# Two-layer hybrid encoder: the gate's first 1024 columns, not 512, with tokens on partitions

## The chip, the core and the metric

The kernel runs on one core of a Trainium2 chip. Its time is the device time of one execution in microseconds, of which the median of three is given; beside it one execution was recorded by the profiler. The core has a matrix engine (TensorE, "PE" in the profile, with its weight loads apart as "PEld"), VectorE ("DVE"), ScalarE ("ACT"), GpSimd ("POOL") and SyncE ("SP"), which here only issues DMAs.

## The reference, cut to what matters

Two layers, each of three sub-layers on a residual stream of 256 tokens by 1024: token mixing, cross-attention into 256 memory tokens, and a gated feed-forward with a depthwise convolution of width 3 over the tokens. The change is in the third:

```python
def conv_ffn(h, w_up, conv_w, conv_b, w_down):      # h 256x1024, w_up 1024x5632, w_down 2816x1024
    a = h @ w_up
    a = conv3(a, conv_w) + conv_b                   # along the tokens, each column by itself
    g, u = jnp.split(a, 2, axis=-1)                 # gate: columns 0..2815, value: 2816..5631
    return (jax.nn.gelu(g, approximate=True) * u) @ w_down
...
h = rms_norm(x, ffn_pre_g[l])
x = x + rms_norm(conv_ffn(h, ...), ffn_post_g[l])
```

## The kernel before

All matrix products are done on split numbers: a weight or an activation is held as a high part (`wh`, `hTH`) and a low part (`wl`, `hTL`), and a product is the sum of three, high by high, high by low and low by high. `wunit` loads 512 KB of weights into a `raw` buffer; ScalarE writes the high part (L139), VectorE the low part (L140). There are six buffers each of `raw`, `wh` and `wl`, so a unit's parts can be made only when the unit six before it has been used up.

`hT` is the normed input turned, with features on partitions: 8 pieces of 128 features by 256 tokens, high and low. The tokens are in two blocks of 128, called block 0 and block 1. At the end of the sub-layer before, `nat_full` finishes block 0, norms it (`add_and_norm`, `prenorm`) and turns it (`raw_T`, L204) while block 1 is still in the product; then the same for block 1.

The feed-forward's up-projection comes in two forms.

- **Tokens on partitions** (`product`, `nat_chunk`, `mm_nat`; L270, L272, L274): 512 columns of the gate at a time. A piece of `hT` of one block is the stationary operand, 512 weight columns move. One block takes 24 matmuls of 512 columns. It needs one block alone, so block 0 can be done before block 1 is turned. The result has tokens on partitions, and the convolution wants them along the free axis, so `first_up` copies it to SBUF (L144) and turns it with four PE transposes a block (L918) into two accumulators, `first[0]` and `first[1]`, of 256 columns of the gate each.
- **Columns on partitions** (the loop over `j`; L943, L944): for 256 columns of gate (`s_` = 0) or value (`s_` = 1), 16 pairs of matmuls: the high weights against high and low tokens at once (512 columns moving), the low weights against the high tokens (256). It needs both blocks. ScalarE (L945) and VectorE (L946) add the two halves into an SBUF tile.

The loop has 11 steps, `j` = 0, 2, ... 20, of a gate half and a value half. At `j` = 0 and 2 the gate half is ready in `first`, so TensorE does the value half alone. For each half the convolution follows: one ScalarE instruction (L950) and two VectorE instructions (L952, L953) for each 128 columns, then gelu (L955), the product of the halves (L956) and the split for the down-projection (L139, L140 on `t`).

Accumulators are PSUM banks: four with the name `acc`, three `att`, one `fil`. Every accumulator of the up-projection is one of the four `acc`. A bank can be written again only when its last reader is done: for the loop's, L946; for `first`, the last L953 of its two.

The strings in `FFN`, one per layer, give the order in which the steps ahead of the loop are written: `uL` loads the units of the 512 columns, `uM0` and `uM1` are their products for the blocks, `e0` and `e1` are `first_up`, `cw` loads the convolution's weights and turns them (L906), `pl` and `p` load and compute a piece of the next layer's memory keys (layer 0 only; its matmuls are L270 to L279 with `fil`). A scheduler then sets the order of instructions on each engine from this, once, at build time; SP's order is that of the text. Each engine runs its own list strictly in that order, so an instruction that waits holds up all behind it on its engine.

Of the kernel before, what the change touches and what calls it, by code (L numbers as in the profile page):

```python
# [21 lines left out]
P = 128  # L22
D = 1024
S = 256
NB = S // P
# [23 lines left out]

MIX = (
# [9 lines left out]
    "g2",  # L62
    "aL aM a0 bL bM b0 A0 a1 pl B0 pr p b1 B1 A1 x1 x0 pl x2 y1 y2 y0 x3 z2 z0 y3 p g2 g0 z1 z3 pg g1 g3")
FFN = (
    "pl uL p uM0 uM1 cw e0 e1",
    "uL cw uM0 e0 uM1 e1")
BUFS = {"t4": 16, "t2": 10, "raw": 6, "w": 6, "acc": 4, "att": 3, "fil": 1, "gB": 2}

ENG = {"mrow": "A", "mT": "V", "dval": "A", "dn": "A", "dTq": "A", "dTk": "A", "kT": "A", "kn": "V",
# [5 lines left out]
def encoder(ctx, tc, a, out):  # L75
# [205 lines left out]
    def blk(b):  # L281
        return slice(b * P, (b + 1) * P)
# [108 lines left out]
    class Memory:  # L391
# [7 lines left out]
        def load(self):  # L399
            mem = a["mem"].rearrange("o (b p) d -> p (o b) d", p=P)  # L400
            self.rows = [t4() for _ in range(NB)]
            for b in range(NB):
                nc.sync.dma_start(self.rows[b], mem[:, b, :])
# [106 lines left out]
    for l in range(DEPTH):  # L510
# [406 lines left out]
                o = (i % 2) * S + b * P  # L917
                T.transpose(st.first[i // 2][:, o:o + P], an[:, blk(i)], ident)  # L918

        load("u", w, 0, 512, 2, None)  # L920
        product("u", 512, 2)
        steps.update(cw=conv_weights, e0=partial(first_up, 0), e1=partial(first_up, 1))
        issue(FFN[l], steps)
        cw, first = st.cw, st.first
        guH, guL = [], []
        for j in range(0, NF, 2):
            if j % 4 == 0:
                guH.append(t4(F32R).rearrange("p (k t) -> p k t", t=S))
                guL.append(t4(F32R).rearrange("p (k t) -> p k t", t=S))
            gu = []  # L930
            for s_ in range(2):
                if j < 4 and s_ == 0:
                    srcs = [first[j // 2][:, m * S:(m + 1) * S] for m in range(2)]
                else:


                    us = [wunit(w[k * P:(k + 4) * P, s_ * D_FF + j * P:s_ * D_FF + (j + 2) * P], 4, 256) for k in (0, 4)]
                    both = t2().rearrange("p (k t) -> p k t", t=S)
                    srcs = [both[:, m, :] for m in range(2)]
                    for m, acc in enumerate(accs()):  # L940
                        for kt in range(KD):
                            wH, wL = us[kt // 4]
                            T.matmul(acc, wH[:, kt % 4, blk(m)], hT[:, kt, :, :], start=kt == 0, stop=False)  # L943
                            T.matmul(acc[:, :S], wL[:, kt % 4, blk(m)], hTH[:, kt, :], start=False, stop=kt == KD - 1)  # L944
                        A_.activation(srcs[m], acc[:, S:], AF.Copy)  # L945
                        V.tensor_tensor(srcs[m], acc[:, :S], srcs[m], op=ALU.add)  # L946
                cv = t2().rearrange("p (k t) -> p k t", t=S)
                taps = [(m, srcs[m], s_ * NF + j + m) for m in range(2)]
                for m, src, f in taps:
                    A_.activation(cv[:, m, :], src, AF.Identity, bias=cw[:, 3, f:f + 1], scale=cw[:, 1, f:f + 1])  # L950
                for m, src, f in taps:
                    V.scalar_tensor_tensor(cv[:, m, 1:], src[:, :S - 1], cw[:, 0, f:f + 1], cv[:, m, 1:], op0=ALU.mult, op1=ALU.add)  # L952
                    V.scalar_tensor_tensor(cv[:, m, :S - 1], src[:, 1:], cw[:, 2, f:f + 1], cv[:, m, :S - 1], op0=ALU.mult, op1=ALU.add)  # L953
                gu.append(cv)
            A_.activation(gu[0], gu[0], AF.Gelu_apprx_tanh)  # L955
            V.tensor_tensor(gu[0], gu[0], gu[1], op=ALU.mult)  # L956
            split(guH[j // 4][:, j % 4:j % 4 + 2, :], guL[j // 4][:, j % 4:j % 4 + 2, :], gu[0])
# [28 lines left out]
```

## Time and profile before

| | |
|---|---|
| device time, median of 3 runs | 851.68 us (850.91 to 852.28) |
| the profiled execution: its time, its span | 851.3 us, 849.5 us |
| TensorE busy, share of the span | 98% |
| VectorE, ScalarE, GpSimd | 74%, 64%, 5% |
| memory read | 139.74 MB, 166 GB/s over the span |
| mean granted TensorE clock | 0.997 |

Matmuls overlap one another, and their ends are modelled, so TensorE's pace is read from one start to the next. The other engines' pace is read in the same way where the list is unbroken.

### The profile page before, as it was taken

The page shows a single profiled execution, that of the slowest core. Times are in us where ns is not written, and L with a number is a line of the kernel's source. Part 1 is how long each engine was busy: PE and PEld are TensorE (multiplying, and loading weights), DVE is VectorE, ACT ScalarE, POOL GpSimd, SP SyncE. Part 2 cuts the span into 40 slices and gives each one's busy share as a digit, 9 for nine tenths or more (in the row PEclk, how much of TensorE's full clock was granted, in tenths as well). Part 3 has the DMA queues.
Part 4 walks back from the last instruction along what each step waited for, and adds up shares of the span by engine and source line. Part 5 has one row for each costly group of instructions (what it writes and reads, how often), then busy time and mean ns, then how long its engine had stood idle before and what let it go on. Part 6 is the DMA issues. An engine that isn't in the chain of part 4 may idle for free.

```text
span 849.5 us, 13117 instructions
## 1 busy us (share of the span) xinstructions
PE 833.2 (98%) x4846; PEld 728.4 (86%) x4846; DVE 625.5 (74%) x1127; ACT 546.9 (64%) x1027; POOL 39.1 (5%) x65
## 2 busy tenths in 40 slices
PE   7999999999999999999999999999998999999997
PEld 5898999889888888888889989988996888888885
DVE  6798664776488999974487787548566799999543
ACT  7798663766368777763376777547636587777331
POOL 1120000100020000000010100001001000000000
PEclk9999999999999999999999999999999999999999
DMA  7873533572355667655737723256624446775531
GB/s 276 275 228 104 166 100 100 156 251 90 94 160 173 201 208 212 203 173 193 219 116 216 236 82 124 76 148 219 191 62 148 154 148 199 223 218 184 183 109 50
DMA packets 94704, 141.64 MB, mean 167 GB/s; under 512 B 5806, under 2 KB 71172, under 8 KB 94640
## 3 DMA queue, kind: packets, MB, share of 16 engines
q1 hardware_dynamic: 94368, 140.59, 52.8%
q8 instruction: 38, 0.62, 0.3%
q14 instruction: 26, 0.21, 0.1%
q0 software_dynamic: 160, 0.18, 0.1%
q10 hardware_dynamic: 112, 0.03, 0.0%
HBM read 139.74 MB, written 1.05 MB: 166 GB/s over the span
## 4 chain that ended last, share of the span: by engine, by line
PE 91%; DVE 4%; POOL 1%; issue 1%; DMA 1%; ACT 1%; SPq 0%; DVEq 0%; POOLq 0%; ACTq 0%
PE acc L943 18%; PE acc L270 13%; PE acc L272 13%; PE acc L274 13%; PE acc L944 9%; PE fil L270 2%; PE fil L274 2%; PE fil L272 2%; PE fil L277 2%; PE att L484 2%; PE fil L278 2%; PE fil L279 2%; PE acc L770 2%; PE acc L782 2%; PE acc L638 1%; PE att L204 1%
## 5 line engine op out<-in xcount | busy, mean ns | idle before, releaser
L140 DVE TENSOR_TENSOR wl<-raw,wh 128x1024 fp32r<-128x1024 f32 (+1 forms) x206 | 249.7, 1215 | 119.9 <-ACT wh L139 118.2
L139 ACT ACTIVATE wh<-raw 128x1024 fp32r<-128x1024 f32 (+1 forms) x206 | 215.6, 1051 | 129.6 <-PE acc L274 85.8
L943 PE MATMUL acc<-hT,wh 128*128 128x512 f32 x640 | 224.3, 396 | 0.0
L944 PE MATMUL acc<-hT,wl 128*128 128x256 f32 x640 | 178.8, 279 | 0.0
L943 PEld LDWEIGHTS acc<-hT,wh 128*128 128x128 f32 x640 | 120.2, 188 | 28.7
L272 PE MATMUL acc<-wl,hT 128*128 128x512 f32 (+3 forms) x384 | 134.9, 373 | 0.0
L274 PE MATMUL acc<-wh,hT 128*128 128x512 f32 (+3 forms) x384 | 134.4, 372 | 0.3 <-DVE hT L140 0.3
L270 PE MATMUL acc<-wh,hT 128*128 128x512 f32 (+3 forms) x384 | 134.7, 375 | 0.0
L944 PEld LDWEIGHTS acc<-hT,wl 128*128 128x128 f32 x640 | 120.7, 189 | 0.0
L274 PEld LDWEIGHTS acc<-wh,hT 128*128 128x128 f32 x384 | 72.7, 190 | 12.2 <-DVE hT L140 1.4
L272 PEld LDWEIGHTS acc<-wl,hT 128*128 128x128 f32 x384 | 72.6, 190 | 11.8 <-DVE wl L140 0.7
L270 PEld LDWEIGHTS acc<-wh,hT 128*128 128x128 f32 x384 | 72.3, 190 | 11.4 <-ACT hT L139 0.4
L270 PE MATMUL acc<-wh,t 128*128 128x512 f32 (+1 forms) x216 | 67.7, 387 | 0.0
L272 PE MATMUL acc<-wl,t 128*128 128x512 f32 (+1 forms) x216 | 67.5, 386 | 0.0
L274 PE MATMUL acc<-wh,t 128*128 128x512 f32 (+1 forms) x216 | 67.0, 384 | 0.0
L950 ACT ACTIVATE t<-t,cw 128x256 f32<-128x256 f32 x80 | 47.5, 595 | 13.9 <-DVE t L946 13.4
L262 ACT ACTIVATE wh<-raw,pre_cols 128x512 fp32r<-128x512 f32 (+3 forms) x80 | 43.7, 616 | 11.9 <-PE acc L274 7.8
L263 DVE SCALAR_TENSOR_TENSOR wl<-raw,pre_cols,wh 128x512 fp32r<-128x512 f32 (+3 forms) x80 | 46.1, 621 | 4.5 <-ACT wh L262 4.5
L270 PEld LDWEIGHTS acc<-wh,t 128*128 128x128 f32 x216 | 39.9, 188 | 8.2 <-issue 0.7
L274 PEld LDWEIGHTS acc<-wh,t 128*128 128x128 f32 x216 | 40.4, 188 | 7.5
L272 PEld LDWEIGHTS acc<-wl,t 128*128 128x128 f32 x216 | 40.3, 188 | 7.6 <-DVE ropeB L372 0.3
L178 POOL TENSOR_TENSOR rstd<-ms,nhalf 128x1 f32<-128x1 f32 x18 | 14.7, 819 | 605.0 <-DVE ms L176 600.4
(189 smaller groups left out, 1397.8 us busy)
## 6 DMA issues: line engine op xcount, KB each, us to landing
raw<-in_ffn_w_up SPq DMA_DIRECT2D x88, 512.0 KB, 4.6
raw<-in_ffn_w_down SPq DMA_DIRECT2D x44, 512.0 KB, 3.4
raw<-in_mem_w_kv SPq DMA_DIRECT2D x32, 512.0 KB, 3.7
raw<-in_w_in SPq DMA_DIRECT2D x20, 512.0 KB, 4.8
raw<-in_w_mix_out SPq DMA_DIRECT2D x16, 512.0 KB, 3.4
raw<-in_mem_w_q SPq DMA_DIRECT2D x16, 512.0 KB, 3.9
raw<-in_mem_w_o SPq DMA_DIRECT2D x16, 512.0 KB, 4.3
raw<-in_w_in SPq DMA_DIRECT2D x8, 384.0 KB, 4.6
```

Of the source, the lines that this page charges most:

```text
L139: return (A_.activation(h, src, AF.Copy), V.tensor_tensor(lo, src, h.bitcast(F32), op=ALU.subtract))
L140: V.tensor_tensor(lo, src, h.bitcast(F32), op=ALU.subtract))
L262: A_.activation(h[:, v], raw[:, v], AF.Copy, scale=g[:, i:i + 1])
L263: V.scalar_tensor_tensor(lo[:, v], raw[:, v], g[:, i:i + 1], h[:, v].bitcast(F32), op0=ALU.mult, op1=ALU.subtract)
L270: T.matmul(o, sH, w, start=start, stop=False)
L272: T.matmul(o, sH, w, start=False, stop=False)
L274: T.matmul(o, sL, w, start=False, stop=stop)
L277: T.matmul(o, wH, sH, start=start, stop=False)
L278: T.matmul(o, wH, sL, start=False, stop=False)
L943: T.matmul(acc, wH[:, kt % 4, blk(m)], hT[:, kt, :, :], start=kt == 0, stop=False)
L944: T.matmul(acc[:, :S], wL[:, kt % 4, blk(m)], hTH[:, kt, :], start=False, stop=kt == KD - 1)
L950: A_.activation(cv[:, m, :], src, AF.Identity, bias=cw[:, 3, f:f + 1], scale=cw[:, 1, f:f + 1])
```

## The change

The gate's columns 512 to 1023 get the first form too. They are a second chunk, called `y`: `yL`, `yM0` and `yM1` are its load and its products, `f0` and `f1` (`next_up`) copy each block's result to SBUF, where it stays in two `t2` tiles (`later`). When the loop comes to `j` = 4 and `j` = 6 it takes one `acc` bank, turns the 256 columns into it with four transposes, and the convolution reads that bank; TensorE does the value half alone there. The number of DMAs and their bytes are as before; four DMAs a layer are of 128x2x512 in place of 128x4x256.

```diff
 FFN = (
-    "pl uL p uM0 uM1 cw e0 e1",
-    "uL cw uM0 e0 uM1 e1")
+    "pl uL yL p uM0 yM0 f0 cw uM1 e0 yM1 e1 f1",
+    "uL yL cw uM0 yM0 f0 uM1 e0 yM1 e1 f1")
...
+        st.later = [None] * NB
+
+        def next_up(b):
+            st.later[b] = t2()
+            copy("up", st.later[b], st.y[b])
+
+        for i, name in enumerate("uy"):
+            load(name, w, i * 512, 512, 2, None)
+            product(name, 512, 2)
...
-                if j < 4 and s_ == 0:
-                    srcs = [first[j // 2][:, m * S:(m + 1) * S] for m in range(2)]
+                if j < 8 and s_ == 0:
+                    if j < 4:
+                        acc = first[j // 2]
+                    else:
+                        acc, = accs(1)
+                        for m in range(2):
+                            for b in range(NB):
+                                T.transpose(acc[:, m * S + b * P:m * S + (b + 1) * P], st.later[b][:, blk(j - 4 + m)], ident)
+                    srcs = [acc[:, m * S:(m + 1) * S] for m in range(2)]
                 else:
```

Lines of the changed kernel are one higher than before up to the steps named, and 16 higher in the loop: L943 and L944 become L959 and L960, L946 becomes L962, L952 and L953 become L968 and L969, L956 becomes L972; the new transposes are L948, those of `first_up` L919.

What follows is the order in which instructions stand on an engine, before and after. It is a list without times.

TensorE in layer 1, where block 1 of the normed input is turned (`att_1429`, `att_1430`); `acc_1448` and `acc_1449` are `first`, `acc_1447` is block 1's product of `u`, and `att_1444` the convolution's weights. Before:

```order
L274 MATMUL acc_1446_7153<-wh_1441_7139,hT_80 128x512
L204 MATMUL att_1429_7105<-ident_72,t4_1424_7094 128x128 x4
L918 MATMUL acc_1448_7179<-ident_72,t2_1450_7181 128x128
L204 MATMUL att_1430_7112<-ident_72,t4_1424_7094 128x128 x4
L906 MATMUL att_1444_7146<-ident_72,t2_1443_7143 128x44 x4
L918 MATMUL acc_1448_7179<-ident_72,t2_1450_7181 128x128
...
L270 MATMUL acc_1447_7154<-wh_1432_7121,hT_80 128x512
```

After, where `acc_1458` and `acc_1459` are the products of `u`, and `acc_1460` that of `y` for block 0:

```order
L275 MATMUL acc_1458_7163<-wh_1441_7125,hT_80 128x512
L273 MATMUL acc_1460_7189<-wl_1445_7132,hT_80 128x512
L205 MATMUL att_1429_7091<-ident_72,t4_1424_7080 128x128 x4
L205 MATMUL att_1430_7098<-ident_72,t4_1424_7080 128x128 x4
L907 MATMUL att_1456_7156<-ident_72,t2_1455_7153 128x44 x4
L275 MATMUL acc_1460_7189<-wh_1444_7131,hT_80 128x512
...
L275 MATMUL acc_1460_7189<-wh_1447_7137,hT_80 128x512
L271 MATMUL acc_1459_7164<-wh_1432_7107,hT_80 128x512
```

Eleven products of `y` for block 0 now stand with the turning of block 1, ten of them between it and the first product that needs it; one more stands some 20 matmuls earlier, between the first two products of `u` and the third. The transposes of `first_up` stand behind block 1's products.

VectorE in the loop of layer 1, from the last L953 (now L969) on `first[1]` to the fourth pass. Before, `acc_1473` and `acc_1474` are the value half of `j` = 2, `acc_1485` and `acc_1486` the gate half of `j` = 4:

```order
L953 SCALAR_TENSOR_TENSOR t2_1465_7288<-acc_1449_7180,cw_1445_7151,t2_1465_7288 128x255
L946 TENSOR_TENSOR t2_1472_7307<-acc_1473_7308,t2_1472_7307 128x256
L946 TENSOR_TENSOR t2_1472_7307<-acc_1474_7309,t2_1472_7307 128x256
L140 TENSOR_TENSOR wl_1493_7426<-raw_1491_7423,wh_1492_7425 128x1024
L140 TENSOR_TENSOR t4_1453_7218<-t2_1454_7219,t4_1452_7217 128x512
L952 SCALAR_TENSOR_TENSOR t2_1475_7346<-t2_1472_7307,cw_1445_7151,t2_1475_7346 128x255 x2
L953 SCALAR_TENSOR_TENSOR t2_1475_7346<-t2_1472_7307,cw_1445_7151,t2_1475_7346 128x255 x2
L946 TENSOR_TENSOR t2_1484_7371<-acc_1485_7372,t2_1484_7371 128x256
```

After, from the same point (`acc_1489` and `acc_1490` are the value half of `j` = 2, `acc_1494` the turned gate columns of `j` = 4, `acc_1503` its value half):

```order
L962 TENSOR_TENSOR t2_1488_7371<-acc_1490_7373,t2_1488_7371 128x256
L141 TENSOR_TENSOR wl_1513_7518<-raw_1511_7515,wh_1512_7517 128x1024
L141 TENSOR_TENSOR t4_1469_7282<-t2_1470_7283,t4_1468_7281 128x512
L968 SCALAR_TENSOR_TENSOR t2_1491_7410<-t2_1488_7371,cw_1457_7161,t2_1491_7410 128x255 x2
L969 SCALAR_TENSOR_TENSOR t2_1491_7410<-t2_1488_7371,cw_1457_7161,t2_1491_7410 128x255 x2
L968 SCALAR_TENSOR_TENSOR t2_1495_7428<-acc_1494_7423,cw_1457_7161,t2_1495_7428 128x255
L972 TENSOR_TENSOR t2_1481_7352<-t2_1481_7352,t2_1491_7410 128x512
L969 SCALAR_TENSOR_TENSOR t2_1495_7428<-acc_1494_7423,cw_1457_7161,t2_1495_7428 128x255
L968 SCALAR_TENSOR_TENSOR t2_1495_7428<-acc_1494_7423,cw_1457_7161,t2_1495_7428 128x255
L141 TENSOR_TENSOR t4_1469_7282<-t2_1481_7352,t4_1468_7281 128x512
L969 SCALAR_TENSOR_TENSOR t2_1495_7428<-acc_1494_7423,cw_1457_7161,t2_1495_7428 128x255
L962 TENSOR_TENSOR t2_1502_7447<-acc_1503_7448,t2_1502_7447 128x256
```

The first rows are the same; then the convolution of the turned columns comes in, and its last instruction on `acc_1494` stands behind the end of the step `j` = 2.

TensorE in the loop of layer 1, with the engines that an instruction waits for. Before, at the start of `j` = 4:

```order
L944 MATMUL acc_1474_7309<-hT_80,wl_1471_7304 128x256
L943 MATMUL acc_1485_7372<-hT_80,wh_1479_7361 128x512 [waits DVE_49]
L944 MATMUL acc_1485_7372<-hT_80,wl_1480_7362 128x256
L943 MATMUL acc_1485_7372<-hT_80,wh_1479_7361 128x512
L944 MATMUL acc_1485_7372<-hT_80,wl_1480_7362 128x256
```

After, at the start of `j` = 6 (`acc_1506` holds its turned columns, `acc_1515` its value half):

```order
L960 MATMUL acc_1504_7449<-hT_80,wl_1501_7444 128x256
L948 MATMUL acc_1506_7497<-ident_72,t2_1462_7215 128x128 [waits DVE_49]
L948 MATMUL acc_1506_7497<-ident_72,t2_1467_7279 128x128
L948 MATMUL acc_1506_7497<-ident_72,t2_1462_7215 128x128
L948 MATMUL acc_1506_7497<-ident_72,t2_1467_7279 128x128
L959 MATMUL acc_1515_7522<-hT_80,wh_1509_7511 128x512 [waits DVE_49,PE_49,Activation_49]
```

Before, `acc_1485` gets the bank that the value half of `j` = 0 had left. After, in the program as built, `acc_1515` gets the bank of `acc_1494`, `acc_1503` that of `first[1]`; in layer 0 the banks follow one another in the same way.

## Rows read from the trace of the kernel before

**Rows 1.** The page: busy time of TensorE; the chain that ended last, by engine.

```profile
PE 833.2 (98%) x4846; PEld 728.4 (86%) x4846; DVE 625.5 (74%) x1127; ACT 546.9 (64%) x1027; POOL 39.1 (5%) x65
...
PE 91%; DVE 4%; POOL 1%; issue 1%; DMA 1%; ACT 1%; SPq 0%; DVEq 0%; POOLq 0%; ACTq 0%
```

**Rows 2.** Waits of TensorE, whole span: in total, times, longest.

```profile
PE att L204 <- DVE t L196: 2.6, 3, 1.7
...
PE acc L918 <- ACT t L144: 0.2, 1, 0.2
```

**Rows 3.** Busy time by stretch: loop layer 0, turn of layer 1, loop layer 1.

```profile
259.90:373.00 113.10, 113.10 (x644) 98.17 (x643) 105.68 (x183) 85.96 (x143) 0.00 (x0) 1.00 0.64 197
...
657.50:660.20 2.70, 2.67 (x7) 2.15 (x8) 2.70 (x4) 1.40 (x4) 0.83 (x2) 0.53 0.32 105
...
672.30:784.00 111.70, 111.70 (x646) 97.63 (x645) 106.07 (x184) 86.76 (x146) 0.00 (x0) 1.00 0.65 200
```

**Rows 4.** Timeline of TensorE, layer 0, from block 1's products into the loop.

```profile
253.00 0.40 PE L270 MATMUL acc<-wh,hT 128*128 128x512 f32 x1
...
258.24 0.39 PE L274 MATMUL acc<-wh,hT 128*128 128x512 f32 x1
258.56 0.44 PE L906 MATMUL att<-ident,t 44*128 44x44 f32 x4
258.93 0.66 PE L918 MATMUL acc<-ident,t 128*128 128x128 f32 x4
...
260.21 0.39 PE L943 MATMUL acc<-hT,wh 128*128 128x512 f32 x1
...
372.57 0.40 PE L943 MATMUL acc<-hT,wh 128*128 128x512 f32 x1
```

**Rows 5.** Timeline of TensorE, layer 1, from block 0's products through the loop.

```profile
657.53 0.79 PE L274 MATMUL acc<-wh,hT 128*128 128x512 f32 x1 [0.30 <-DVE hT L140]
...
660.17 0.39 PE L274 MATMUL acc<-wh,hT 128*128 128x512 f32 x1
...
663.83 0.60 PE L204 MATMUL att<-ident,t 128*128 128x128 f32 x4
664.67 0.33 PE L918 MATMUL acc<-ident,t 128*128 128x128 f32 x1 [0.25 <-ACT t L144]
...
666.05 0.47 PE L270 MATMUL acc<-wh,hT 128*128 128x512 f32 x1
...
671.60 0.39 PE L943 MATMUL acc<-hT,wh 128*128 128x512 f32 x1
...
673.29 0.40 PE L943 MATMUL acc<-hT,wh 128*128 128x512 f32 x1
...
782.84 0.40 PE L943 MATMUL acc<-hT,wh 128*128 128x512 f32 x1
```

**Rows 6.** Timeline of VectorE, layer 1, the loop's first steps.

```profile
677.59 1.23 DVE L140 TENSOR_TENSOR wl<-raw,wh 128x1024 fp32r<-128x1024 f32 x1 [0.97 <-ACT wh L139]
...
683.29 0.68 DVE L956 TENSOR_TENSOR t<-t,t 128x512 f32<-128x512 f32 x1
683.88 0.47 DVE L953 SCALAR_TENSOR_TENSOR t<-acc,cw,t 128x255 f32<-128x255 f32 x1
684.28 0.74 DVE L946 TENSOR_TENSOR t<-acc,t 128x256 f32<-128x256 f32 x2
684.94 1.21 DVE L140 TENSOR_TENSOR wl<-raw,wh 128x1024 fp32r<-128x1024 f32 x1
686.07 0.69 DVE L140 TENSOR_TENSOR t<-t,t 128x512 fp32r<-128x512 f32 x1
686.67 0.87 DVE L952 SCALAR_TENSOR_TENSOR t<-t,cw,t 128x255 f32<-128x255 f32 x2
687.46 0.87 DVE L953 SCALAR_TENSOR_TENSOR t<-t,cw,t 128x255 f32<-128x255 f32 x2
688.25 0.42 DVE L946 TENSOR_TENSOR t<-acc,t 128x256 f32<-128x256 f32 x1
```

**Rows 7.** Timeline of ScalarE, layer 1: a weight unit whose buffers TensorE held.

```profile
676.50 1.06 ACT L139 ACTIVATE wh<-raw 128x1024 fp32r<-128x1024 f32 x1 [0.88 <-PE acc L943]
```

**Rows 8.** One line's instructions, the transposes of `first_up`: duration ns min/median/max.

```profile
L918 PE MATMUL acc<-ident,t x16: 270/273/332, 258.9 to 672.8; 128*128 128x128 f32 x16
```

More of the change, by code (lines that the diff above doesn't have):

```diff
@@ L918, in first_up @@
                 T.transpose(st.first[i // 2][:, o:o + P], an[:, blk(i)], ident)
-        load("u", w, 0, 512, 2, None)
-        product("u", 512, 2)
-        steps.update(cw=conv_weights, e0=partial(first_up, 0), e1=partial(first_up, 1))
+        st.later = [None] * NB
[5 more added lines that the diff above has]
+            product(name, 512, 2)
+        steps.update(cw=conv_weights, f0=partial(next_up, 0), f1=partial(next_up, 1), e0=partial(first_up, 0), e1=partial(first_up, 1))
         issue(FFN[l], steps)
```

## The prediction

> **What bounds the kernel now.** I read the page first, then the chain that ended last, the waits of TensorE, the windows, and last the timelines of the two places that the change touches. On the page TensorE is busy for 98% of the span, and 91% of the chain is its own [rows 1]; so the time is TensorE's list plus its waits. In its waits one group in the touched part is worth something, the turning of the normed blocks (L204), 2.6 us in three waits over all, and one of 0.2 us at L918 [rows 2]. The loop's matmuls, L943 and L944, have no wait at all. The windows say the same of the loop: TensorE is busy for 113.10 of 113.10 us in layer 0 and 111.70 of 111.70 in layer 1 at a granted clock of 1.00, VectorE for 105.68 and 106.07 [rows 3]. So VectorE has some 6% to spare over the loop, and what counts is whether it is late at one point of it. Block 0's products in layer 1 ran at a granted clock of 0.53 [rows 3].
>
> **The change, TensorE's own work.** A layer loses the gate halves of `j` = 4 and 6: 2 x 16 = 32 pairs of L943 and L944. In layer 0, pair 1 starts at 260.21 and pair 319 at 372.57 [rows 4]: 112.36/318 = 0.3533 us a pair, so 32 are 11.31 us. In layer 1, pair 3 at 673.29 and pair 319 at 782.84 [rows 5]: 109.55/316 = 0.3467, so 11.09 us. It gains two blocks of 24 matmuls of 512 columns. Those of block 1 in layer 0 start from 253.00 to 258.24 [rows 4], 23 steps of 0.2278 us; 48 are 10.93 us. The columns that move are as many (24,576 each way), which the near equality bears out.
>
> It gains 8 transposes a layer, in two sets of four. From the first of eight at 258.93 to the loop's first pair at 260.21 are 1.28 us [rows 4], and the later of these starts is one pair in, so the eight take 1.28 - 0.353 = 0.93 us, a set 0.47, one 0.117. By columns alone (a quarter of 0.2278) one would be 0.057 and the eight 0.46; I take the measured starts and keep 0.47 less a layer as the lower end. Net: layer 0 -11.31 + 10.93 + 0.93 = +0.55 us, layer 1 -11.09 + 10.93 + 0.93 = +0.77.
>
> The Trainium skill ("TensorE: Matmul & The Clock Gate", Part 4: PE-mode transpose) gives about 275 ns for one such transpose in a kernel. As a duration the trace agrees, 273 ns [rows 8], but their starts are closer together than that; which of the two counts is rival D.
>
> Four ScalarE copies (L945) and four VectorE additions (L946) a layer go too; behind a TensorE without waits they were worth nothing before. The DMAs move the same bytes, no more of them, and the loads of `y` are issued where there is no wait for data, so I put 0.
>
> **The weight buffers ahead of the loop.** There are six. `u`'s four units and `y`'s first two fill them; `y`'s third and fourth units can be split only when block 1's products have let go of the first two. From that release follow the high part, 1.06 us on ScalarE, which elsewhere too stands behind a matmul [rows 7], and the low part, 1.23 on VectorE behind it [rows 6], with the steps between them some 2.7 us; between release and need TensorE has 12 matmuls, 12 x 0.2278 = 2.73 us. It is about even: 0.2 us a layer (0 to 0.6).
>
> **The waits that are covered.** In layer 1 ten of block 0's products of `y` stand between the turning of block 1 and the first product that needs it. From the last turns at 663.83 to that product at 666.05 are 2.22 us [rows 5]. In them lie twelve transposes of 128 columns at 0.117 and the four of L906, which took 0.37 in layer 0 (258.56 to 258.93 [rows 4]): 1.77 us of own work, so 0.45 of wait goes, the 0.25 at L918 among it. One `y` matmul fills 0.23 of the gap of 0.30 at 657.53 [rows 5]. From the loop's first pair at 671.60 to pair 3 at 673.29 are 1.69 us, in which three pairs and four transposes make 1.04 + 0.47; the other 0.18 are behind `first_up`, which now has products ahead of it. In all -0.86 us (-0.5 to -1.4, if the own work in that stretch is smaller). VectorE and ScalarE turn the blocks in the same order as before, so the rest of the waits at L204 stays. In layer 0 no such wait is in the rows, so 0. Without what follows the sum is 0.55 + 0.2 = +0.75 us in layer 0 and 0.77 + 0.2 - 0.86 = +0.11 in layer 1.
>
> **The banks in the loop, the main term.** Before, TensorE spent 11.1 us on each pass from `j` = 4 on; now the passes 4 and 6 are, like 0 and 2, half as long, and VectorE must keep up with four short ones in a row. An `acc` bank is free when its last reader is done. The value half of `j` = 6 gets the bank in which the gate columns of `j` = 4 were turned, and its reader is the last L969 on `acc_1494`, which stands far down VectorE's list.
>
> *When VectorE gets there.* The list is the same as before up to the point at which L946 stood at 688.25 in layer 1 [rows 6], and it was unbroken. The loop began at 673.29 - 3 x 0.3467 = 672.25 [rows 5], so this is 16.0 us into it. From there I add steps of the same rows [rows 6], start to start: L968 0.40, L972 0.60, L969 0.40, L968 0.40, the split of `t` (L141) 0.60, and L969 till its end 0.48: 16.0 + 2.88 = 18.9. L141 waits for ScalarE's high part of the same `t`, which follows the product by L972: I take 0.25 us more, the lower end being 0 and the upper 1.0 (about one ScalarE instruction of rows 7 that comes in between): 19.15.
>
> *When TensorE gets there.* Without a stall it has three short passes and two sets of transposes behind it: in layer 1 3 x 16 x 0.3467 + 2 x 0.47 = 17.58 us, in layer 0 3 x 16 x 0.3533 + 0.94 = 17.90. So it waits 19.15 - 17.58 = 1.55 us in layer 1 and 1.25 in layer 0 (1.3 and 1.0 without the wait for ScalarE, 2.3 and 2.0 with all of it). A smaller wait comes first and is in this sum, not beside it: `acc_1503` gets the bank of `first[1]`, whose last L953 begins at 683.88 [rows 6] and ends at 684.35, 12.1 us in, against 11.1 + 0.47 = 11.56 for TensorE. What is queued behind the waiting matmul is all of TensorE, nothing else can go on there; VectorE and ScalarE work on and catch up.
>
> *What is late next.* The loop's 106 us of VectorE are nine full passes and two short ones, which lack two low parts (L140, 1.13 each) and two L946 (0.33 each): 10.2 us for a full pass, 7.25 for a short one. TensorE takes 11.1 and 5.55. After the wait the next thing that VectorE must deliver is the low part of the second unit of `j` = 8. TensorE needs it one short pass and eight pairs later, at 19.15 + 5.55 + 2.77 = 27.5 us; VectorE has a short pass and the low part ahead of it, 19.15 + 7.25 + 1.13 = 27.5. It is even, and I put 0; from there each full pass gives VectorE 0.9 us.
>
> **The sum.** 0.75 + 1.25 + 0.11 + 1.55 = 3.66 us. The profiled execution took 851.3 us, which gives 855.0; the median of the runs is 0.4 above that execution, less than the measurement tells. 0.2% of the time, 1.7 us, is about what it can tell from no change: "the same" is 850.0 to 853.4.
>
> **The rivals.**
>
> A, *the banks are not late*: VectorE gets through its list sooner than the list of before suggests, since four L946 fewer stand in it and it is no longer behind units that TensorE holds. For it: in the rows VectorE had 0.97 us of wait at 677.59 behind ScalarE, which was behind TensorE [rows 6, 7]. Against: that wait lies ahead of the point from which I count, in a stretch whose order doesn't change. Sum +0.86: 852.2 (851.0 to 853.3).
>
> B, *VectorE stays behind after `j` = 8*: with no margin at `j` = 8 a low part late by 0.1 to 0.3 us in each of the seven passes left, in both layers, costs about 2 x 7 x 0.18 = 2.5 us more: 857.5. Against: a full pass gives VectorE 0.9 us back.
>
> C, *the half-rate stretch goes away*, on the other side. In layer 1 the six steps from 657.53 to 660.17 took 0.44 us each [rows 5] where 0.23 is the pace at a clock of 1.00: 1.2 us lost. The engine had waited just before (the waits of the turn [rows 2]), and one `y` matmul now stands in that gap. If it keeps the clock up, that is -1.2 us. It decides only where A holds as well, and the transposes and the covered waits are at their favourable ends: 0.86 - 0.94 - 0.54 - 1.2 = -1.8, so 849.5. Against: the longest wait ahead of it, 1.7 us, stays as it is.
>
> D, *a transpose counts with its whole duration*: the 16 new ones at 0.273 [rows 8] in place of 0.117 are +2.5 us: 857.5. Against: eight took 0.93 us [rows 4]. This is the time by the figure of the skill page named above; the rows on starts speak against it.
>
> That the change doesn't do what it says has no chance of its own: the built order has 288 pairs a layer in the loop, where before it had 320.
>
> **How the numbers follow.** The forecast (waits on banks, 853.4 to 856.5) gets 0.58, A 0.21, B 0.13, C 0.05, D 0.03. The range runs from A's middle part to B's time, 851.8 to 857.5: it leaves out C (0.05), part of A (0.06) and the upper half of B and D (0.08). Faster is C, 0.05. The same is nearly all of A, 0.21. Slower is the rest: 0.58 + 0.13 + 0.03 = 0.74.
>
> **What the profile after would show.** Among TensorE's waits there would be a new group, L959 behind VectorE, once or twice a layer at 11.6 and 17.6 us into the loop, 1 to 2 us a layer in all; none of it at L960 or later passes. The pace stays 0.35 us a pair, 576 pairs of L959 and 16 transposes of L948 with some 0.12 us from start to start. VectorE's busy time falls by about 3 us (eight L946 of 0.33 are 2.6). The wait of 0.25 us at the transposes of `first_up` is gone. The forecast is wrong if no wait stands at L959 (A), if L959 and L960 wait in each pass (B), if the stretch of block 0's products in layer 1 has a granted clock of 1.00 (C), or if the four L948 of a set take over 1 us (D). It is also wrong if the third and fourth units of `y` come more than 0.6 us late, which would show as a wait of L271 or L273 behind ScalarE or VectorE.

## The result, and the profile after

The changed kernel took 857.02 us in the median of four runs (855.8 to 858.03) against 851.50 for the kernel before beside it: a ratio of 1.0063, 95% interval 1.005 to 1.0076. Measured again later, the same program took 856.65 against 852.59, 1.0041 (1.0028 to 1.0055). The 17 executions of the kernel before in that second measurement fall into two groups, nine at 851.1 to 852.6 (median 851.64) and eight at 853.4 to 854.1; against the lower group the change is 5.0 us. So by the two ratios it is slower by 3.5 to 5.4 us; 855.0 was forecast, within 851.8 to 857.5. The profiled execution took 855.8 us with a span of 853.9, 4.4 more than before.

The page after the change, TensorE's busy time and the chain by engine, to hold against [rows 1]:

```profile
PE 834.3 (98%) x4830; PEld 727.3 (85%) x4830; DVE 621.6 (73%) x1119; ACT 547.0 (64%) x1023; POOL 38.6 (5%) x65
...
PE 88%; DVE 6%; ACT 2%; POOL 2%; issue 1%; DMA 1%; SPq 0%; DVEq 0%; POOLq 0%; ACTq 0%
```

Busy time hides what happened: TensorE gained 1.1 us, VectorE lost 3.9, and the chain moved by 3% of the span away from TensorE, 2% of it to VectorE. The waits of TensorE, to hold against [rows 2] (in total, times, longest), have the new group:

```profile
PE att L205 <- DVE t L197: 2.8, 4, 1.7
PE acc L959 <- DVE t L969: 1.9, 3, 0.9
PE acc L959 <- ACT wh L140: 0.9, 1, 0.9
...
PE acc L275 <- DVE hT L141: 0.3, 1, 0.3
```

TensorE's timeline after the change shows where they stand; the first and last rows of each layer bound the stages used below.

```profile
241.03 0.66 PE L205 MATMUL att<-ident,t 128*128 128x128 f32 x4 [0.66 <-DVE t L197]
...
272.40 0.40 PE L959 MATMUL acc<-hT,wh 128*128 128x512 f32 x1
...
283.36 0.60 PE L948 MATMUL acc<-ident,t 128*128 128x128 f32 x4
284.41 0.47 PE L959 MATMUL acc<-hT,wh 128*128 128x512 f32 x1 [0.46 <-DVE t L969]
...
284.84 0.40 PE L959 MATMUL acc<-hT,wh 128*128 128x512 f32 x1
...
290.14 0.60 PE L948 MATMUL acc<-ident,t 128*128 128x128 f32 x4
291.64 0.47 PE L959 MATMUL acc<-hT,wh 128*128 128x512 f32 x1 [0.91 <-DVE t L969]
...
374.97 0.39 PE L959 MATMUL acc<-hT,wh 128*128 128x512 f32 x1
...
657.40 1.38 PE L205 MATMUL att<-ident,t 128*128 128x128 f32 x8 [1.74 <-DVE t L197]
...
659.98 0.50 PE L275 MATMUL acc<-wh,hT 128*128 128x512 f32 x1 [0.28 <-DVE hT L141]
...
684.79 0.40 PE L959 MATMUL acc<-hT,wh 128*128 128x512 f32 x1
...
695.54 0.60 PE L948 MATMUL acc<-ident,t 128*128 128x128 f32 x4
696.70 0.47 PE L959 MATMUL acc<-hT,wh 128*128 128x512 f32 x1 [0.56 <-DVE t L969]
...
702.43 0.60 PE L948 MATMUL acc<-ident,t 128*128 128x128 f32 x4
703.95 0.47 PE L959 MATMUL acc<-hT,wh 128*128 128x512 f32 x1 [0.92 <-ACT wh L140]
...
787.25 0.39 PE L959 MATMUL acc<-hT,wh 128*128 128x512 f32 x1
```

The fourth wait is put down to ScalarE. VectorE's timeline at the same places tells who it was:

```profile
283.79 0.48 DVE L969 SCALAR_TENSOR_TENSOR t<-acc,cw,t 128x255 f32<-128x255 f32 x1
...
291.02 0.48 DVE L969 SCALAR_TENSOR_TENSOR t<-acc,cw,t 128x255 f32<-128x255 f32 x1
...
696.08 0.47 DVE L969 SCALAR_TENSOR_TENSOR t<-acc,cw,t 128x255 f32<-128x255 f32 x1
...
702.72 0.69 DVE L141 TENSOR_TENSOR t<-t,t 128x512 fp32r<-128x512 f32 x1 [0.41 <-ACT t L140]
703.33 0.48 DVE L969 SCALAR_TENSOR_TENSOR t<-acc,cw,t 128x255 f32<-128x255 f32 x1
```

These L969 end at 284.27, 291.50, 696.55 and 703.81, and TensorE goes on 0.14, 0.14, 0.15 and 0.14 us later: all four waits end by the last reader of the bank, at the forecast place. The high part that ScalarE ends at 703.96 beside the last wait isn't the one that `acc_1515` needs, since TensorE went on at 703.95.

The two loops (first and last row) and block 0's products in layer 1, by windows, to hold against [rows 3]:

```profile
271.70:375.40 103.70, 102.34 (x590) 89.45 (x589) 99.07 (x175) 81.72 (x137) 0.00 (x0) 1.00 0.63 193
659.90:662.70 2.80, 2.72 (x12) 2.27 (x13) 2.80 (x5) 1.21 (x3) 0.85 (x2) 1.00 0.39 123
684.40:787.60 103.20, 101.72 (x587) 88.91 (x586) 98.86 (x175) 81.67 (x136) 0.00 (x0) 1.00 0.63 196
```

By this count each loop now has 1.4 to 1.5 us in which TensorE stands, and the stretch that ran at a granted clock of 0.53 before has 1.00 here.

Cut at such rows, every trace falls into the same stages. For before, the two rows that are not yet shown:

```profile
240.57 0.66 PE L204 MATMUL att<-ident,t 128*128 128x128 f32 x4 [0.67 <-DVE t L196]
...
654.95 1.38 PE L204 MATMUL att<-ident,t 128*128 128x128 f32 x8 [1.74 <-DVE t L196]
```

"Ahead" runs from the first turn of the feed-forward (240.57, 654.95) to the loop's second pair, "loop" from there to the start of the last pair; the kernels are those of the experiments below.

| us | start to the turn | ahead, layer 0 | loop, layer 0 | ahead, layer 1 | loop, layer 1 |
|---|---|---|---|---|---|
| before | 240.57 | 19.64 | 112.36 | 16.99 | 110.90 |
| before, second trace | 242.18 | 19.64 | 112.36 | 16.01 | 110.89 |
| after | 241.03 | 31.37 | 102.57 | 27.39 | 102.46 |
| after, second trace | 241.64 | 31.45 | 102.39 | 27.61 | 102.58 |
| layer 0 alone | 241.58 | 31.45 | 102.39 | 16.06 | 113.00 |
| layer 1 alone | 241.69 | 19.64 | 112.36 | 27.96 | 104.30 |
| turned into att | 242.99 | 31.39 | 102.67 | 27.61 | 102.46 |
| spaced | 242.75 | 31.39 | 101.96 | 27.91 | 101.51 |
| one tap less | 241.48 | 31.37 | 101.92 | 27.62 | 101.94 |
| before, two and two | 241.21 | 19.45 | 110.86 | 15.88 | 111.42 |
| after, two and two | 240.84 | 31.24 | 102.32 | 27.29 | 102.91 |

Layer 0 costs 31.37 + 102.57 - 19.64 - 112.36 = +1.94 us, layer 1 +1.96, and 0.46 came before the change began: that column goes from 240.6 to 243.0 over programs whose TensorE lists are the same up to there.

### The profile page after: what moved, and what is told of

It is laid out like the page before. It is cut to its first block, busy times and chain, and to the rows that moved or that the text cites. A ratio compares the mean times of both kernels' runs of the same rounds, so it can differ in the third digit from the quotient of the medians.

```text
span 853.9 us, 13063 instructions
## 1 busy us (share of the span) xinstructions
PE 834.3 (98%) x4830; PEld 727.3 (85%) x4830; DVE 621.6 (73%) x1119; ACT 547.0 (64%) x1023; POOL 38.6 (5%) x65
## 4 chain that ended last, share of the span: by engine, by line
PE 88%; DVE 6%; ACT 2%; POOL 2%; issue 1%; DMA 1%; SPq 0%; DVEq 0%; POOLq 0%; ACTq 0%
PE acc L959 14%; PE acc L271 14%; PE acc L273 14%; PE acc L275 14%; PE acc L960 7%; PE fil L271 2%; PE fil L275 2%; PE fil L273 2%; PE fil L278 2%; PE att L485 2%; PE fil L279 2%; PE fil L280 2%; PE acc L771 2%; PE acc L783 2%; PE acc L639 1%; PE att L205 1%
## 5 line engine op out<-in xcount | busy, mean ns | idle before, releaser
L141 DVE TENSOR_TENSOR wl<-raw,wh 128x1024 fp32r<-128x1024 f32 (+1 forms) x206 | 249.5, 1214 | 127.0 <-ACT wh L140 125.6
L959 PE MATMUL acc<-hT,wh 128*128 128x512 f32 x576 | 201.1, 394 | 2.8 <-DVE t L969 1.9
L960 PE MATMUL acc<-hT,wl 128*128 128x256 f32 x576 | 160.5, 280 | 0.0
L273 PE MATMUL acc<-wl,hT 128*128 128x512 f32 (+3 forms) x416 | 147.0, 374 | 0.0
L275 PE MATMUL acc<-wh,hT 128*128 128x512 f32 (+3 forms) x416 | 146.4, 372 | 0.3 <-DVE hT L141 0.3
L271 PE MATMUL acc<-wh,hT 128*128 128x512 f32 (+3 forms) x416 | 146.4, 376 | 0.0
L959 PEld LDWEIGHTS acc<-hT,wh 128*128 128x128 f32 x576 | 107.6, 187 | 27.4 <-ACT t L961 3.7
L960 PEld LDWEIGHTS acc<-hT,wl 128*128 128x128 f32 x576 | 108.7, 189 | 0.9
L273 PEld LDWEIGHTS acc<-wl,hT 128*128 128x128 f32 x416 | 78.2, 188 | 13.9 <-DVE wl L141 1.5
L275 PEld LDWEIGHTS acc<-wh,hT 128*128 128x128 f32 x416 | 78.3, 188 | 13.1 <-DVE hT L141 1.1
L271 PEld LDWEIGHTS acc<-wh,hT 128*128 128x128 f32 x416 | 77.7, 189 | 12.9 <-ACT wh L140 0.9
L966 ACT ACTIVATE t<-t,cw 128x256 f32<-128x256 f32 x72 | 42.2, 595 | 8.1 <-DVE t L962 7.4
```

The lines of the kernel that those rows point to most:

```text
L141: V.tensor_tensor(lo, src, h.bitcast(F32), op=ALU.subtract))
L271: T.matmul(o, sH, w, start=start, stop=False)
L273: T.matmul(o, sH, w, start=False, stop=False)
L275: T.matmul(o, sL, w, start=False, stop=stop)
```

## The experiments

**The change again, in layer 0 alone, and in layer 1 alone.** For the parts, `FFN` keeps the old string for the other layer, and (shown for layer 0 alone; layer 1 alone has `l == 1`):

```diff
-        for i, name in enumerate("uy"):
+        for i, name in enumerate("uy"[:1 + (l == 0)]):
...
-                if j < 8 and s_ == 0:
+                if j < (8 if l == 0 else 4) and s_ == 0:
```

> The changed kernel again, to have a second trace of it. It took 857.0 us in the median and 855.8 in its profiled execution, in which block 0's products of layer 1 ran at a granted clock of 1.00. Theory (banks): four waits at L959, two a layer, of 0.4 to 0.6 and 0.9 us, each ending 0.14 us after an L969 has ended, in any execution; median 856 to 858. Rival (clock): the profiled execution was short because the half-rate stretch of layer 1 was missing, and a second trace has it, with a granted clock near 0.53 there and 1.2 us more; then the median of 857.0 is the profiled time plus that stretch. Rival (pace): no such stretch, but pairs of the loop at 0.353 us in place of 0.350, which over 576 pairs is 1.7 us.

> The change in layer 0 alone; layer 1 as before. By the traces layer 0 is +2.0 us (forecast +2.0), so 853.5 us. If the two layers' shares were not added up (a stretch that starts earlier meets other transfers), it would be within 0.5 us of 851.5, or over 855.

> The change in layer 1 alone; layer 0 as before. By the traces layer 1 is +2.0 us, with a half-rate stretch of 1.2 us that was in the trace of before and missing after (forecast +1.7 without that): 853.5 us. If the stretch stays in most executions, as the rival on the clock has it, layer 1 costs +3.2 us: 854.7.

Measured: 856.65 (ratio above); layer 0 alone 853.99, 1.002 (1.0007 to 1.0033); layer 1 alone 856.28, 1.0038 (1.0025 to 1.0052), beside 852.59 for before. The second trace has its four waits at the same matmuls (0.47, 0.94, 0.42, 0.92), so they belong to the program and not to one execution. The half-rate stretch of layer 1 is there this time:

```profile
660.40:663.10 2.70, 2.70 (x9) 2.09 (x8) 2.70 (x5) 1.03 (x3) 0.94 (x2) 0.65 0.32 99
```

It comes and goes with the execution (absent in the second trace of before too, 16.01 against 16.99), not with the change: of the fourteen traces 2 of the 7 with the old order of layer 1 have it and 5 of the 7 with the new one. With `y` it costs less: 27.61 (granted clock 0.65) and, with layer 1 alone, 27.96 (0.52) against 27.39. Like for like layer 1 is +2.3 us (both with it) or +2.95 (both without).

Against the lower group of before, layer 0 alone is +2.3 us where +2.0 was expected, and layer 1 alone +4.6 where 2.0 to 3.2 was; together they are 2 us more than the whole change. The table shows where the traced executions lost it. With layer 1 alone its loop took 104.30 and not 102.46: a further wait of 0.58 at a low part (L960), and the pairs behind it slower. With layer 0 alone the traced execution (855.39, in a spread of 852.7 to 857.3) had a loop of layer 1 of 113.00 in place of 110.90, though TensorE's last 2,981 instructions, by tile and shape, stand in the order of before. The windows in that loop (40 us of unbroken pairs, the first bracket counts TensorE's instructions), of before and of it:

```profile
320.00:360.00 40.00, 40.00 (x228) 34.71 (x228) 38.08 (x67) 29.62 (x49) 0.00 (x0) 1.00 0.67 209
730.00:770.00 40.00, 40.00 (x232) 34.97 (x231) 38.67 (x66) 30.23 (x51) 0.00 (x0) 1.00 0.69 210
```

```profile
320.00:360.00 40.00, 40.00 (x233) 35.28 (x232) 39.59 (x67) 31.64 (x52) 0.00 (x0) 1.00 0.74 223
730.00:770.00 40.00, 40.00 (x229) 34.68 (x228) 38.18 (x66) 30.25 (x51) 0.00 (x0) 1.00 0.68 209
```

The pairs have two paces, 0.353 and 0.347 us, both at a granted clock of 1.00, and nothing that a wait shows lies between them.

**The turned columns in another bank.**

```diff
-                        acc, = accs(1)
+                        acc = psum1()
```

> The turned columns of j = 4 and 6 go to one of the three att banks, which the loop doesn't use, in place of an acc bank. Theory (banks): the value halves no longer wait for the last L969 of a gate, so the four waits at L959 go (1.4 and 1.5 us a layer) with the 0.25 us that TensorE needs to start again after each; 853.1 to 854.1 us, unless VectorE is late with a low part at j = 8, where a wait at L960 would give back up to 1.2 us a layer (855 to 856). Rival (weights): the row of layer 1 names ScalarE's high part L140; if that is what was late, 0.9 us of wait stays at L959 in layer 1 and as much in layer 0: 855.5 or more. Rival (elsewhere): the waits are not where the time went, 857 with no wait in the loop.

Measured: 858.58 us, 1.0067 (1.0054 to 1.0081). The waits at L959 are gone, and in their place:

```profile
PE acc L960 <- DVE wl L141: 3.0, 4, 0.8
```

As much as the 2.8 of before this edit, two a layer, one in each half of `j` = 8, and the loops are as long (102.67, 102.46). The bank was only where VectorE's lateness showed first; my theory named the wait rightly and its cause too narrowly, and both of its times were missed. Both rivals fall: no wait stayed at L959, and there were waits. The median is 1.9 us over that of the changed kernel with the `acc` bank, and not by the feed-forward: the two traced executions are 2.4 apart, 1.35 of it ahead of the turn and 1.1 behind the last matmul. Whether that belongs to this program stays open.

**The short passes apart, and less work for VectorE in them.** First the chunk `y` from column 1024, then the third tap left out on the gate of `j` = 0 to 6:

```diff
-            load(name, w, i * 512, 512, 2, None)
+            load(name, w, i * 1024, 512, 2, None)
...
-                if j < 8 and s_ == 0:
+                if j in (0, 2, 8, 10) and s_ == 0:
...
-... st.later[b][:, blk(j - 4 + m)], ident)
+... st.later[b][:, blk(j - 8 + m)], ident)
```

```diff
-                    V.scalar_tensor_tensor(cv[:, m, :S - 1], src[:, 1:], cw[:, 2, f:f + 1], ...
+                    if j >= 8 or s_ == 1:
+                        V.scalar_tensor_tensor(cv[:, m, :S - 1], src[:, 1:], cw[:, 2, f:f + 1], ...
```

> The changed kernel with the second chunk moved from the gate's columns 512 to 1023 to its columns 1024 to 1535, so that the short passes are j = 0, 2, 8 and 10, with the full passes j = 4 and 6 between them. As much work, as many transposes, as many banks. Theory (VectorE falls behind over four short passes in a row, the bank is only where it shows first): each full pass gives VectorE 0.9 us back, so the waits of 1.4 to 1.5 us a layer shrink to under 0.4, and with the restarts 853.5 to 854.5 us against 856.7. Rival (the wait is the bank's, wherever the turned columns use it): the same two waits a layer at j = 8 and 10, 856.5.

> The changed kernel without the third tap of the convolution (L969) on the gate's columns of j = 0 to 6, which leaves out part of the computation: two instructions of 0.39 us less for VectorE in each of the four short passes, 3.2 us a layer; TensorE's work is the same. Theory (VectorE's work in the short passes): it was about 1.5 us late, so all waits in the loop go, and with the restarts 853 to 854 us against 856.7. Rival (a fixed wait of a bank or for ScalarE): some 0.9 us of wait a layer stays.

Measured: spaced 855.18, 1.0038 (1.0026 to 1.005); one tap less 855.07, 1.0035 (1.0022 to 1.0048), beside 851.99. The waits of the spaced kernel, and all that are left with one tap less:

```profile
PE acc L960 <- DVE wl L141: 1.8, 2, 0.9
```

```profile
PE att L205 <- DMA x<-in_x: 6.5, 2, 3.7
PE att L205 <- DVE t L197: 2.6, 3, 1.8
PE att L414 <- ACT t L145: 0.5, 1, 0.5
```

With two full passes between, the wait shrinks from 1.4 to 0.89 a layer, more than the 0.4 that I had put, and stands at a low part of `j` = 12, behind the short passes, not at the bank. With 3.2 us less for VectorE a layer there is none. So the wait comes from VectorE being late after short passes in a row, and less work for it removes it. VectorE isn't busy all the time before it is late: in layer 1 of the changed kernel it waited 2.4 us for ScalarE in the first 9 us of the loop, and then its list was unbroken from 693.41 to 702.31:

```profile
685.75 0.48 DVE L968 SCALAR_TENSOR_TENSOR t<-acc,cw,t 128x255 f32<-128x255 f32 x1 [0.58 <-ACT t L966]
...
689.79 1.22 DVE L141 TENSOR_TENSOR wl<-raw,wh 128x1024 fp32r<-128x1024 f32 x1 [0.78 <-ACT wh L140]
...
692.50 0.42 DVE L962 TENSOR_TENSOR t<-acc,t 128x256 f32<-128x256 f32 x1 [0.57 <-ACT t L961]
693.41 0.48 DVE L968 SCALAR_TENSOR_TENSOR t<-acc,cw,t 128x255 f32<-128x255 f32 x1 [0.49 <-ACT t L966]
```

The kernel before has four such waits there too (0.62, 0.97, 0.57, 0.49). No run took work from ScalarE, so what ScalarE adds to the lateness is not shown.

But both kernels were to come to 853 to 854.5, and the loops became shorter by only 0.5 to 1.0 us. With one tap less the loop of layer 0 is 101.92 = 286 x 0.3533 + 2 x 0.43: no wait, and every pair at the slower pace. In the changed kernel the pairs run at 0.347 from about 320 us on. Without the wait this is gone too. TensorE's order differs as well: in the changed kernel the scheduler put high products two in a row in three places near `j` = 8 and 10, and with one tap less the alternation is unbroken. Which of the two the pace followed is not shown.

The trace with one tap less also tells how to read a wait. Its pair behind a set starts 0.35 us after the set's first transpose, while the four transposes last 0.60 together:

```profile
283.80 0.60 PE L948 MATMUL acc<-ident,t 128*128 128x128 f32 x4
284.15 0.48 PE L959 MATMUL acc<-hT,wh 128*128 128x512 f32 x1
...
284.59 0.40 PE L959 MATMUL acc<-hT,wh 128*128 128x512 f32 x1
```

A row of waits counts from the end of the 0.60, so behind a set it is 0.25 us short of what the wait costs.

**The price of a set of transposes.** The kernel before, with `an` kept in `st.later`, and ahead of the gate halves of `j` = 4 to 18:

```diff
+                    if 4 <= j < 20 and s_ == 0:
+                        spare = psum1()
+                        for i in range(4):
+                            T.transpose(spare[:, blk(i)], st.later[i % 2][:, blk(i)], ident)
```

> The kernel before with 8 sets of four transposes a layer in the loop, one ahead of the gate half of each of j = 4 to 18, into an att bank that nothing reads; they add no work to VectorE. Forecast (0.47 a set by start to start): 16 sets, +7.5 us, 859 to 860. Rival (whole duration of 0.273 each): +17.5 us, 869. Rival (columns alone, 0.057 each): +3.6 us, 855. If each set also costs a restart of the pair behind it, as the starts of the changed kernel suggest (0.35 and 0.08), 0.43 a set: +6.9. By the theory of two paces the pairs may change from 0.353 to 0.347 after a set, which would take back up to 2 us in layer 0.

Measured: 861.02 us against 851.99. Two sets in a row, with 32 pairs between their starts:

```profile
272.85 0.60 PE L942 MATMUL att<-ident,t 128*128 128x128 f32 x4
...
284.59 0.60 PE L942 MATMUL att<-ident,t 128*128 128x128 f32 x4
```

11.74 - 32 x 0.3533 = 0.43 us a set, the slower pair behind it included, as the last of the expected prices had it; the loop of layer 0 grew by 8 x 0.43 = 3.46 (115.82). The measured 9.0 is over the forecast of 6.9 to 7.5: the rest is layer 1's loop, 116.27, which left 0.347 for 0.353 at its first set. The Trainium skill ("TensorE: Matmul & The Clock Gate", Part 4: PE-mode transpose) has about 275 ns for one of bf16 in a kernel; here 0.27 is the duration of one, and four in a row take 0.43, the slower pair behind them included.

**What sets the pace.** The kernel before once more, and with the loop's products in another order: two exchanged once in each layer, two and two throughout, and the low ones one later. The middle one:

```diff
...
-                        for kt in range(KD):
-                            wH, wL = us[kt // 4]
-                            T.matmul(acc, wH[:, kt % 4, blk(m)], hT[:, kt, :, :], start=kt == 0, stop=False)
-                            T.matmul(acc[:, :S], wL[:, kt % 4, blk(m)], hTH[:, kt, :], start=False, stop=kt == KD - 1)
+                        for kt in range(0, KD, 2):
+                            high(kt)
+                            high(kt + 1)
+                            low(kt)
+                            low(kt + 1)
```

> The kernel before again, for a second trace of it. Its 17 runs beside the last experiments fall in two groups, 851.1 to 852.6 and 853.4 to 854.1. In the traces so far a pair of the loop takes either 0.347 or 0.353 us for a whole stretch: 0.353 in layer 0 of both kernels with the loop of before there, 0.347 in layer 1 of before, 0.353 in layer 1 of the kernel that changes layer 0 alone. Theory (two paces): layer 0 at 0.353 again; layer 1 at 0.347 (time 851 to 852) or at 0.353 (320 pairs by 0.0065, 2.1 us, more: 853.4 to 854). Rival: the groups come from the start, the 96 products of the first 40 us, which differed by up to 1.4 us between traces, and the paces stay as they were.

> The kernel before with two matmuls exchanged once in each layer: at the loop's first half the high products of the first two pieces come in a row, then the two low ones, and from there on the two alternate as before. In the traces so far the pairs changed from 0.353 to 0.347 us in the changed kernel behind the places where such doubles stand (near j = 8), and never within an unbroken alternation. Theory (the pace is set where the alternation starts, and keeps): layer 0 goes to 0.347, 2.1 us less, 849.5 us; layer 1 may go the other way (2.1 more). Rival (the pace goes with the layer's place or its buffers): 0.353 and 0.347 as before, 851.6.

> The kernel before with the loop's matmuls two and two throughout: two high products, two low ones. As many matmuls and columns. Theory (the pace is set where a run of one kind starts): with a fresh start at every double the pairs have one pace in both layers; if it is 0.347, 849.5 us, if 0.353, 853.7. Rival (two low products in a row wait for their weight loads, since 256 columns are over before a load of 0.19 us is): up to 0.08 us a pair slower, over 870.

> The kernel before with each low product one high product later than it was, so that every half ends with two low ones and begins with two high ones. Theory (the pace is set at each start): one pace in both layers, chosen anew in each half, 849.5 if it is 0.347 and 853.7 if 0.353, or a mixture. Rival (the pace goes with the layer): 0.353 in layer 0 and 0.347 in layer 1, 851.6.

Measured: before again 851.64, with the two paces as in its first trace. One exchange: 853.78, 1.0018 (1.0008 to 1.0027), and in its trace 0.353 and 0.347 as before, so a double is not enough, and in none of the ten executions is the 849.5 of the theory. The traced execution took 851.53, the other nine 853.1 to 854.7: 2.1 us more would be a layer's 320 pairs at the other pace, which was not traced. The low products one later: 853.47, 1.0019 (1.001 to 1.0028), with 0.3525 in both layers, near the slower pace. Two and two:

```profile
320.00:360.00 40.00, 40.00 (x231) 34.89 (x230) 38.55 (x67) 29.96 (x50) 0.00 (x0) 1.00 0.66 210
730.00:770.00 40.00, 40.00 (x231) 34.89 (x230) 38.64 (x68) 29.83 (x50) 0.00 (x0) 1.00 0.65 210
```

one pace in both layers, 0.348, near the better (the loop of layer 0, cut as in the table, 110.86 us where it was 112.36; layer 1 111.42 where it was 110.90), and 850.55 us, 0.9989 (0.998 to 0.9999): about 1 us ahead of the kernel before, by an interval that barely leaves out no change. The rival on the weight loads falls.

**The change in that order.** The same edit in the changed kernel.

> The changed kernel with the loop's matmuls two and two, as in the run before this one, which had its pairs at 0.348 us in both layers: the change without the pace's share. Theory (terms add up): against that kernel's 850.5 a layer gains 11.75 us (layer 0) or 11.3 (layer 1) of products ahead of the loop, loses 32 x 0.347 = 11.1 of pairs, gains two sets at 0.43, two waits of 1.45 in all with 0.5 of restarts: +3.4 and +3.1, so 857.0 us, with waits of 1.4 to 1.6 a layer at L959's place. Rival (the difference of the two kernels as first measured, 5.0, holds at any pace): 855.5.

Measured: 856.32, 1.0051 (1.0038 to 1.0065) against 851.72. It is 5.8 us above the two-and-two kernel's median of another measurement (5.3 by the two ratios), between the 6.5 of the theory and the 5.0 of the rival, so the medians don't decide. The traces, both with a granted clock of 1.00 in block 0's products, lean to the theory: by the table layer 0 costs 31.24 + 102.32 - 19.45 - 110.86 = +3.25 us and layer 1 +2.90, where +3.4 and +3.1 were expected, and layer 0 cost +1.94 where the pace changed. It is one trace of each. The waits are there, and one more at a low part in layer 1:

```profile
PE acc L958 <- DVE t L976: 2.5, 4, 0.8
...
PE acc L961 <- DVE wl L141: 0.4, 1, 0.4
```

## Why the prediction held, and where its sizes were off

The time fell inside the range, 2.0 us above the forecast in the first measurement. The mechanism was right in the main; two of its terms were too small, and one was put at nothing. The terms by layer, each worked out from the table and the rows above; layer 1 against the second trace of before, since neither has the half-rate stretch:

| us | layer 0 forecast | layer 0 measured | layer 1 forecast | layer 1 measured |
|---|---|---|---|---|
| products ahead of the loop, buffers, covered waits | +11.13 | +11.73 | +10.27 | +10.73 |
| 32 pairs fewer | -11.31 | -11.31 | -11.09 | -11.09 |
| two sets of transposes | +0.93 | +0.86 | +0.93 | +0.86 |
| waits in the loop, start to start | +1.25 | +1.85 | +1.55 | +1.98 |
| pace of the pairs that are left | 0 | -1.2 | 0 | +0.46 |
| sum | +2.00 | +1.93 | +1.66 | +2.94 |

(Layer 1's first term is 27.39 - 16.01 less 0.65, since four transposes of `first_up` stood behind the second pair before: 110.90 - 318 x 0.3467 = 0.65. The last term is what is left of the loop.)

- *The banks, the main term*: right in place and count, too small in size, 2.80 us for 3.83. The sum reckoned a wait from one start to another. Read like that, with 0.35 us from a set's first transpose to a pair that doesn't wait, the four pairs start 0.70 (behind 283.36), 1.15, 0.81 and 1.17 us late. The rows of waits give 2.85 for the four, close to the forecast by chance, since they leave out 0.25 each. VectorE's last L969 on the turned columns ended 19.45 us into the loop of layer 0 (taken to begin at 272.40 - 0.35) and 19.37 into that of layer 1 (684.79 - 0.35), where 19.15 was forecast for both; L141 waited about 0.4 for ScalarE and not 0.25. TensorE went on 0.14 later still, which the sum had left out, and was there 0.16 and 0.05 us sooner than forecast. (The text's 19.15 - 17.58 is 1.57, not 1.55.) The smaller wait came first, as written. The sentence that its reader is the cause was too narrow: with another bank the same time is lost at a low part.
- *The sets*: 0.43 for 0.47.
- *No slow start*: the expectations reckon 0.25 us for TensorE to start again behind a wait. The rows don't bear it out: from the pair behind a wait to the next are 0.43 us (284.41 to 284.84), behind a set without a wait 0.44 (284.15 to 284.59). The 0.25 is the part of the wait that its row doesn't count.
- *The products ahead of the loop*: 0.6 and 0.46 more than forecast, though no product stands waiting for a weight unit, for which 0.2 a layer was in the sum. In layer 0 changes between products and transposes cost about 0.1 each, and there are more of them. In layer 1 the waits that `y` covers are 0.5 + 0.34 without the half-rate stretch, and 0.28 + 0.19 of these stayed.
- *The pace*, put at nothing: "112.36/318 = 0.3533 us a pair" was taken to hold for the pairs that are left. From about 320 us on it was 0.347 in layer 0, and part of layer 1's pairs went to 0.353. By chance this nearly cancels the two terms that were too small in layer 0.
- *The rivals*: A (no waits) is out by the four rows, B (VectorE late in every later pass) by their absence after `j` = 6, D by the set's 0.43. C did happen in the profiled execution, but the stretch is absent in some executions of the kernel before too, so it is no gain of the change.

Of the 5.4 us of the first measurement, some 4.2 to 4.9 are these terms; the rest is within what the start differs between executions.

## What to carry to other kernels

Where a stage's matrix work is shortened on one form and paid back on another, look at what VectorE owes over the next passes, not at the engine's share of the stage: 6% to spare over the whole loop was 1.9 us too little over four short passes. Read a wait from start to start, as the work around it was read: a row of waits that begins at the end of overlapping work leaves a part out. To name the cause of a wait, move it: here another bank only moved it to the next thing that the late engine delivers. And before a gain is worked out from a pace, take that pace from more than one trace.

## What the runs showed of the chip that I had not expected

An unbroken alternation of matmuls of 512 and 256 columns ran at 0.3533 or at 0.3467 us a pair, at a granted clock of 1.00 either way, and kept its pace for up to 110 us. Over a layer's 320 pairs this is 2.1 us, as much as the waits that the change made there (1.85 and 1.98). It changed behind waits, sets of transposes and stretches with doubled matmuls, not always to the better: a set of transposes took layer 1 from 0.347 to 0.353, a wait of 0.58 at a low part did the same in the kernel that changes layer 1 alone, and the stretch near `j` = 8 and 10 of the changed kernel did the reverse. The same order of layer 1 ran at either. Pairs in twos ran at 0.348 in both layers, pairs with the low product one later at 0.3525. What fixes it was not found. The stretch at half rate in layer 1, with a granted clock of 0.52 to 0.65, likewise comes in some executions of one program and not in others.
